# One moving operand of 512 columns for both parts of an activation, and a whole PSUM bank per output tile, in a two-layer decoder trunk

## The chip, the cores and the metric

The kernel runs on one core of a Trainium2 chip. The metric is the device time of one execution in microseconds (us). TensorE (PE in the profile) multiplies, ScalarE (ACT) and VectorE (DVE) do the work on single elements, GpSimd (POOL) builds a few small matrices, and SyncE (SP) issues the transfers. A difference of about 0.2% (1.8 us) is the least that three or more runs of this kernel tell from none.

## The reference

The program is a decoder of two layers over 256 positions and 1024 features. Layer 0 mixes tokens by dilated attention, layer 1 by an mLSTM block. After its mixer every layer runs a squared-ReLU MLP and a gated per-layer embedding:

```
for i in range(DEPTH):
    if i % N_MIXERS == 0:
        x = x + dilated_attention(rms_norm(x, a_norm[j]), ...)     # 9 projections of 1024 x 1024, then w_o
    else:
        x = x + mlstm_mixer(rms_norm(x, b_norm[j]), ...)           # w_up 1024 x 4096, w_down 2048 x 1024
    x = x + squared_relu_mlp(rms_norm(x, mlp_norm[i]), mlp_w1[i], mlp_w2[i])   # relu(h @ w1)**2 @ w2
    gate = jax.nn.sigmoid(rms_norm(x, ple_norm[i]) @ ple_w_gate[i])
    x = x + gate * (p[i] @ ple_w_proj[i])
```

All inputs are fp32, and the result has to be nearly as exact as an fp32 product.

## The kernel before

**Split products.** TensorE works on a short fp32 format (`fp32r`). So each fp32 operand is split into a high part, its rounding, and a low part, the rest, and a product a·w is summed as a_h·w_h + a_l·w_h + a_h·w_l. Weights come from HBM in 138 units of 128 x 2048 (`raw`, 1 MB each). `split` makes `hi` on ScalarE (L176) and `lo` on VectorE (L177), 512 columns at a time. One such piece is called a slot here; a slot holds four weight tiles of 128 x 128, and a unit four slots. `hi` and `lo` are rings of twelve slots, and `split` runs up to 11 slots ahead of the matmuls (`LS`).

**Two kinds of products.** The first 36 units are the attention's q, k and v (`qkv_block`, L499 to L501): there the activation is the stationary operand and 512 weight columns move. The other 102 units are products by `stream`: the weight tile (128 x 128) is stationary and 256 columns of the activation (all positions, features on partitions) move. These 102 units are, in order: proj0 (1 unit), woA and woB (4 together), w1 and w2 of layer 0 (16 each), gate0 (4), xm (8), z0 to z3 (2 each), wd0 (4), proj1 (1), wd1 (4), w1 and w2 of layer 1 (16 each) and gate1 (4). A unit has 16 weight tiles, so there are 1632 of them.

**stream.** For every weight tile it issues three matmuls of 128 x 256 (L331: w_h with a_h; L332: w_h with a_l; L333: w_l with a_h), each with its own weight load. `os` is a pair of output tiles, which share one PSUM bank as `acc[:, 0]` and `acc[:, 1]`; in the last blocks of a few products it is a single tile with half a bank. The pool `psa` has three banks. When a block is done, `done(os, acc)` reads the sum out of PSUM; for pairs that is one operation of 512 columns: `add_x` (wo and wd, L623), `mid` (w1), `fin` (w2, singles), `done` of the gate (L669, held back by `DF` slots for the first outputs, since the norm's factor `rb` is not there yet), `xm_done` (L774) and `done` of z.

**Norms.** `next_h` scales a finished column of x into the next product's activation (`scaled`: `hh` on ScalarE, L298, `hl` on VectorE, L299) and adds its square to the statistics (`Stats`, L264). The factor of the norm is applied after the product, as a row `rb` or `r2` that `rstd_rows` makes six slots (`SB`) into the product.

**Order.** Work that belongs to a later slot is put there by `at`. The order on each engine is made when the kernel is built, by a scheduler that goes by priority: `split` has a low one, `add_x` a high one (`PX`).

Of the kernel before, what the change touches and what calls it, by code (L numbers as in the profile page):

```python
# [39 lines left out]
def _blocks(no, ks, singles=0):  # L40

    n = no - singles
    os = [(o, o + 1) for o in range(0, n, 2)] + [(o,) for o in range(n, no)]
    return [(b, list(ks)) for b in os]

# [94 lines left out]
def _build(ctx, tc, nc, a):  # L140
# [56 lines left out]
    DF = 3  # L197
# [51 lines left out]
    hA = [base.tile([P, KT, S], F32R, name=f"h{n}") for n in "hl"]  # L249
# [68 lines left out]
    def stream(blocks, rhs, done, defer=0):  # L318

        i = 0  # L320
        for os, ks in blocks:
            n = len(os)
            acc = psa.tile([P, n, S], F32, name="acc")
            for k in ks:
                for q, o in enumerate(os):
# [3 lines left out]
                    h, l = rhs(k)  # L329
                    first, last = k == ks[0] and q == 0, k == ks[-1]  # L330
# [12 lines left out]
    def from_h(h):  # L343
        return lambda k: (h[0][:, k], h[1][:, k])
# [730 lines left out]
```

## Time and profile before

| | |
|---|---|
| median of 3 runs | 922.49 us (921.65 to 922.83) |
| the profiled execution | 921.63 us |
| its span, first to last instruction | 919.9 us |
| TensorE busy | 904.3 us, 98% of the span |
| VectorE busy | 659.7 us, 72% |
| ScalarE busy | 569.5 us, 62% |
| mean granted TensorE clock | 0.997 of 2.4 GHz |

The profile shows one execution. A busy time is the time in which at least one instruction of the engine runs; a matmul's duration in it covers the way through the array too, so that consecutive ones overlap, and what a matmul costs in a dense stretch is read from the starts of consecutive ones, not from their durations. For VectorE and ScalarE as well, the next instruction starts about 0.09 us before the one ahead ends.

### The profile page before, as it was taken

How to read it: one execution, taken by the hardware profiler on the slowest of the kernel's cores; microseconds unless marked ns; L12 is line 12 of the kernel's file. 1: busy time of each engine (PE TensorE's matmuls, PEld its weight loads, DVE VectorE, ACT ScalarE, POOL GpSimd, SP SyncE). 2: the span in 40 equal slices, each digit the busy share in tenths (PEclk: the TensorE clock that was granted, in tenths of full speed). 3: DMA queues.
4: the chain of work that ended last, by engine and by line, in shares of the span. 5: the costliest groups of instructions: out<-in, count | busy, mean ns of one | idle time of the engine just before them, and what ended most of it. 6: DMA issues, size and time to landing. Idle time of an engine off the chain costs nothing.

```text
span 919.9 us, 17609 instructions
## 1 busy us (share of the span) xinstructions
PE 904.3 (98%) x6924; PEld 844.3 (92%) x6924; DVE 659.7 (72%) x1409; ACT 569.5 (62%) x1055; POOL 41.5 (5%) x77
## 2 busy tenths in 40 slices
PE   8799999999999999999999999999999999999997
PEld 6687787877889999999999899999999999999997
DVE  6966877857866866665667987568898666656664
ACT  7567576575585766654446686668866666644442
POOL 0400000000000000000000542000000000000000
PEclk9999999999999999999999999999999999999999
DMA  8744443544443555555555433343265555555521
GB/s 302 281 142 160 156 144 133 178 136 145 154 161 105 178 185 183 184 183 184 183 184 183 157 129 104 127 138 98 87 220 204 184 183 184 184 183 182 184 94 46
DMA packets 23122, 150.23 MB, mean 163 GB/s; under 512 B 2560, under 2 KB 3200, under 8 KB 5632
## 3 DMA queue, kind: packets, MB, share of 16 engines
q1 hardware_dynamic: 23040, 149.12, 47.1%
q8 instruction: 54, 0.88, 0.4%
q14 instruction: 28, 0.23, 0.1%
HBM read 148.06 MB, written 1.05 MB: 162 GB/s over the span
## 4 chain that ended last, share of the span: by engine, by line
PE 92%; DVE 6%; ACT 1%; issue 1%; DMA 0%; SPq 0%; ACTq 0%
PE acc L331 21%; PE acc L332 21%; PE acc L333 21%; PE acc L499 6%; PE acc L501 6%; PE acc L500 6%; DVE lo L177 2%; PE tp L451 1%; PE tp L552 1%; PE sm L570 1%; PE sc L527 1%; PE tp L741 1%; PE tp L751 1%; PE sc L882 1%; PE sc L759 1%; PE sc L533 1%
## 5 line engine op out<-in xcount | busy, mean ns | idle before, releaser
L177 DVE TENSOR_TENSOR lo<-raw,hi 128x512 fp32r<-128x512 f32 x552 | 375.6, 691 | 176.7 <-ACT hi L176 175.3
L176 ACT ACTIVATE hi<-raw 128x512 fp32r<-128x512 f32 x552 | 339.2, 628 | 227.1 <-PE acc L332 204.4
L331 PE MATMUL acc<-hh,hi 128*128 128x256 f32 x640 | 184.0, 288 | 0.3 <-ACT hh L298 0.2
L332 PE MATMUL acc<-hl,hi 128*128 128x256 f32 x640 | 181.5, 284 | 0.1
L333 PE MATMUL acc<-hh,lo 128*128 128x256 f32 x640 | 181.4, 283 | 0.0
L331 PE MATMUL acc<-hidh,hi 128*128 128x256 f32 x512 | 144.9, 283 | 0.0
L332 PE MATMUL acc<-hidl,hi 128*128 128x256 f32 x512 | 144.9, 283 | 0.0
L333 PE MATMUL acc<-hidh,lo 128*128 128x256 f32 x512 | 144.9, 283 | 0.0
L331 PEld LDWEIGHTS acc<-hh,hi 128*128 128x128 f32 x640 | 122.4, 191 | 1.6 <-issue 0.7
L332 PEld LDWEIGHTS acc<-hl,hi 128*128 128x128 f32 x640 | 122.5, 191 | 0.7 <-DVE hl L299 0.5
L333 PEld LDWEIGHTS acc<-hh,lo 128*128 128x128 f32 x640 | 122.4, 191 | 0.0
L499 PE MATMUL acc<-hi,hh 128*128 128x512 f32 x264 | 109.6, 416 | 0.0
L500 PE MATMUL acc<-lo,hh 128*128 128x512 f32 x264 | 104.1, 394 | 0.8 <-DVE lo L177 0.8
L501 PE MATMUL acc<-hi,hl 128*128 128x512 f32 x264 | 104.2, 395 | 0.0
L331 PEld LDWEIGHTS acc<-hidh,hi 128*128 128x128 f32 x512 | 98.3, 192 | 0.0
L332 PEld LDWEIGHTS acc<-hidl,hi 128*128 128x128 f32 x512 | 98.3, 192 | 0.0
L333 PEld LDWEIGHTS acc<-hidh,lo 128*128 128x128 f32 x512 | 98.3, 192 | 0.0
L331 PE MATMUL acc<-hBh,hi 128*128 128x256 f32 x320 | 90.9, 284 | 0.0
L332 PE MATMUL acc<-hBl,hi 128*128 128x256 f32 x320 | 90.7, 283 | 0.0
L333 PE MATMUL acc<-hBh,lo 128*128 128x256 f32 x320 | 90.6, 283 | 0.0
L331 PEld LDWEIGHTS acc<-hBh,hi 128*128 128x128 f32 x320 | 61.4, 192 | 0.3 <-issue 0.3
L332 PEld LDWEIGHTS acc<-hBl,hi 128*128 128x128 f32 x320 | 61.4, 192 | 0.0
(258 smaller groups left out, 1384.3 us busy)
## 6 DMA issues: line engine op xcount, KB each, us to landing
raw<-w SPq DMA_DIRECT2D x136, 1024.0 KB, 4.9
raw<-w SPq DMA_DIRECT2D x8, 256.0 KB, 6.8
x<-x SPq DMA_DIRECT2D x4, 256.0 KB, 5.4
pj<-rep SPq DMA_DIRECT2D x1, 896.0 KB, 6.9
out<-u SPq DMA_DIRECT2D x3, 256.0 KB, 2.4
pT<-p SPq DMA_DIRECT2D x2, 256.0 KB, 4.0
nd<-nd SPq DMA_DIRECT2D x1, 384.0 KB, 6.2
out<-u SPq DMA_DIRECT2D x2, 128.0 KB, 1.9
```

The lines of the kernel that those rows point to most:

```text
L176: act(hi[n][:, d], raw[u][:, s], AF.Copy)
L177: dve.tensor_tensor(lo[n][:, d], raw[u][:, s], hi[n][:, d], op=ALU.subtract)
L331: mm(acc[:, q], wh, h, start=first, stop=False, skip_group_check=n > 1)
L332: mm(acc[:, q], wh, l, start=False, stop=False, skip_group_check=n > 1)
L333: mm(acc[:, q], wl, h, start=False, stop=last, skip_group_check=n > 1)
L451: nc.tensor.transpose(ps[:, pair, b * P:(b + 1) * P], n[:, b, ty * 256 + pair * P:ty * 256 + (pair + 1) * P], ident)
L499: mm(accs[b], hh, wh, start=(k == 0), stop=False)
L500: mm(accs[b], hh, wl, start=False, stop=False)
L501: mm(accs[b], hl, wh, start=False, stop=(k == 7))
L527: mm(ps[:, 0:256], q[r, pair, tb], k[r, pair], start=first, stop=last)
L533: mm(ps[64 * e:64 * e + 64, 256 + 64 * n:320 + 64 * n], QT[qt, g][0][r, pair, t4], KTt[qt, g][0][r, pair, t4], start=True, stop=True)
L552: nc.tensor.transpose(psf[:, k * P:(k + 1) * P], pe[:, k * P:(k + 1) * P], ident)
```

## The change

An activation's two parts become one tile with a leading axis of 2 (`parts`): element 0 of what it returns is the whole, 1 the high part, 2 the low part. In `stream` the two matmuls that share w_h become one: w_h is stationary, and both parts move, 2 x 256 columns, into a whole bank; the w_h·a_h sum lands in its first half and the w_h·a_l sum in its second. The third matmul, w_l·a_h, adds to the first half. So each output tile has a bank of its own, and its two halves have to be added when it is read out: `whole` copies the second half to SBUF on ScalarE and adds the first on VectorE, and `add_x` adds one half after the other to x. The blocks are now one pair, whose two banks take turns over k, and then singles (w2 and z: singles alone). Where an operation worked on 512 columns of a pair from PSUM, there is now one of 256 columns per half or per output. In the gate and in xm the read-out no longer waits for `rb`: `whole` is done at once, and the rest (`rest`, `xm_rest`) at slot 6 or later (`late`). Squaring in `mid` moves from ScalarE and VectorE to one VectorE operation (max with 0, times itself), and ScalarE rounds its result. The products of the embeddings (`proj`, 32 weight tiles) keep the old form under the name `stream_pairs`, and q, k and v keep theirs.

```diff
-def _blocks(no, ks, singles=0):
-    n = no - singles
-    os = [(o, o + 1) for o in range(0, n, 2)] + [(o,) for o in range(n, no)]
+def _blocks(no, ks, first=2):
+    os = [tuple(range(first))] + [(o,) for o in range(first, no)]
     return [(b, list(ks)) for b in os]
...
+    def parts(p, name, *shape, **k):
+        t = p.tile([P, 2, *shape], F32R, name=name, **k)
+        return [t, t[:, 0], t[:, 1]]
...
-    def stream(blocks, rhs, done, defer=0):
+    def stream(blocks, h, done):
         i = 0
         for os, ks in blocks:
-            n = len(os)
-            acc = psa.tile([P, n, S], F32, name="acc")
+            accs = [psa.tile([P, 2, S], F32, name="acc") for _ in os]
...
-                    mm(acc[:, q], wh, h, start=first, stop=False, skip_group_check=n > 1)
-                    mm(acc[:, q], wh, l, start=False, stop=False, skip_group_check=n > 1)
-                    mm(acc[:, q], wl, h, start=False, stop=last, skip_group_check=n > 1)
-                    if last and q == n - 1:
-                        if defer and i < 16:
-                            at(clock[0] + defer, done, os, acc)
-                        else:
-                            done(os, acc)
+                    mm(acc.rearrange("p a b -> p (a b)"), wh, h[0][:, :, k], start=first, stop=False, skip_group_check=True)
+                    mm(acc[:, 0], wl, h[1][:, k], start=False, stop=last, skip_group_check=True)
+                    if last:
+                        done(o, acc)
...
+    def late(t0, f, *args):
+        if clock[0] > t0 + SB:
+            f(*args)
+        else:
+            at(t0 + SB, f, *args)
+
+    def whole(out, acc):
+        act(out, acc[:, 1], AF.Copy)
+        dve.tensor_tensor(out, out, acc[:, 0], op=ALU.add)
...
-    def add_x(os, acc):
+    def add_x(o, acc):
         with tc.high_priority(offset=PX):
-            dve.tensor_tensor(x[:, span(os)], x[:, span(os)], acc, op=ALU.add)
+            for n in range(2):
+                dve.tensor_tensor(x[:, o], x[:, o], acc[:, n], op=ALU.add)
...
-            act(u, acc, AF.Relu)
-            s = tmp.tile([P, 2, S], F32, name="s", bufs=2)
-            dve.tensor_tensor(s, u, u, op=ALU.mult)
-            act(hid[0][:, span(os)], u, AF.Square)
-            dve.tensor_tensor(hid[1][:, span(os)], s, hid[0][:, span(os)], op=ALU.subtract)
+            whole(u[:, o % 2], acc)
+            if o % 2:
+                s = tmp.tile([P, 2, S], F32, name="s", bufs=2)
+                dve.scalar_tensor_tensor(s, u, 0.0, u, op0=ALU.max, op1=ALU.mult)
+                act(hid[1][:, o - 1:o + 1], s, AF.Copy)
+                dve.tensor_tensor(hid[2][:, o - 1:o + 1], s, hid[1][:, o - 1:o + 1], op=ALU.subtract)
...
-            dve.tensor_tensor(t, acc[:, 0], r2, op=ALU.mult)
+            whole(t, acc)
+            dve.tensor_tensor(t, t, r2, op=ALU.mult)
...
-            dve.tensor_tensor(t, acc, rb[:, None, :].to_broadcast([P, n, S]), op=ALU.mult)
+            t = tmp.tile([P, S], F32, name="gt", bufs=3)
+            whole(t, acc)
+            late(t0, rest, o, t)
...
-        dve.tensor_tensor(xm, acc, urb[0][:, None, :].to_broadcast([P, 2, S]), op=ALU.mult)
+        whole(xm[:, o % 2], acc)
+        if o % 2 == 0:
+            return
+        late(xm0, xm_rest, o - 1, xm)
```

How the order on the engines changes is shown at three places. The first is TensorE where woB ends and w1 of layer 0 begins. Numbers behind a name tell buffers apart; `oT` is the attention's output, `h` the normed input of w1. Before:

```order
L331 MATMUL acc_3543<-oTh_202,hi_3274 128x256
L332 MATMUL acc_3543<-oTl_203,hi_3274 128x256
L333 MATMUL acc_3543<-oTh_202,lo_3275 128x256
L331 MATMUL acc_3568<-hh_115,hi_3308 128x256 [waits DVE_49,Activation_49]
L332 MATMUL acc_3568<-hl_116,hi_3308 128x256
L333 MATMUL acc_3568<-hh_115,lo_3309 128x256
L331 MATMUL acc_3568<-hh_115,hi_3308 128x256
```

After:

```order
L338 MATMUL acc_3507<-oT_201,hi_3259 128x512
L339 MATMUL acc_3507<-oT_201,lo_3260 128x256
L338 MATMUL acc_3529<-h_115,hi_3292 128x512 [waits DVE_49,PE_49,Activation_49]
L339 MATMUL acc_3529<-h_115,lo_3293 128x256
L338 MATMUL acc_3529<-h_115,hi_3292 128x512 [waits Activation_49]
L339 MATMUL acc_3529<-h_115,lo_3293 128x256
L338 MATMUL acc_3529<-h_115,hi_3315 128x512 [waits DVE_49]
L339 MATMUL acc_3529<-h_115,lo_3316 128x256
L338 MATMUL acc_3530<-h_115,hi_3292 128x512 [waits DVE_49,PE_49]
```

Two matmuls stand for three, the two outputs of the first block have a bank each (3529 and 3530), and the first matmul of a weight tile needs both parts of its column of `h`.

The second place is VectorE at the end of woB: L623 (L656 after) adds a product to x, L299 (L306) makes the low part of `h`, L264 (L271) sums squares, and L177 (L180) is the weights' `lo`. Before:

```order
L177 TENSOR_TENSOR lo<-raw,hi 128x512 [waits Activation_49]
L623 TENSOR_TENSOR x<-x,acc 128x512 [waits PE_49]
L623 TENSOR_TENSOR x<-x,acc 128x256 [waits PE_49]
L299 SCALAR_TENSOR_TENSOR hl<-x,prm,hh 128x256 [waits Activation_49] x2
L264 TENSOR_TENSOR sqa<-sqa,sqt 128x512 [waits Activation_49]
L623 TENSOR_TENSOR x<-x,acc 128x256 [waits PE_49]
L299 SCALAR_TENSOR_TENSOR hl<-x,prm,hh 128x256 [waits Activation_49] x2
```

After:

```order
L656 TENSOR_TENSOR x<-x,acc 128x256 [waits PE_49]
L306 SCALAR_TENSOR_TENSOR h<-x,prm,h 128x256 [waits Activation_49]
L656 TENSOR_TENSOR x<-x,acc 128x256 [waits DVE_49]
L271 TENSOR_TENSOR sqa<-sqa,sqt 128x512 [waits Activation_49]
L306 SCALAR_TENSOR_TENSOR h<-x,prm,h 128x256 [waits Activation_49] x4
L271 TENSOR_TENSOR sqa<-sqa,sqt 128x512 [waits Activation_49]
L180 TENSOR_TENSOR lo<-raw,hi 128x512 [waits DMAHW2_49]
```

Two adds of 256 columns per output stand where one add of 512 served a pair, and the weights' `lo` has moved behind the last `h`.

The third place is VectorE where gate0 ends and xm takes over: L669 (L704 after) multiplies by `rb`, L672 (L707) by the embedding, L697 (L738) adds to x, and L376 is the add of `whole`. Before:

```order
L669 TENSOR_TENSOR u<-acc,rb 128x256 [waits PE_49]
L697 TENSOR_TENSOR xn<-x,u 128x4x4x16 [waits DVE_49]
L177 TENSOR_TENSOR lo<-raw,hi 128x512
L672 TENSOR_TENSOR u<-s,pj 128x256 [waits Activation_49]
L299 SCALAR_TENSOR_TENSOR hl<-xn,prm,hh 128x256 [waits Activation_49]
```

After:

```order
L376 TENSOR_TENSOR gt<-gt,acc 128x256 [waits Activation_49]
L180 TENSOR_TENSOR lo<-raw,hi 128x512
L707 TENSOR_TENSOR gt<-s,pj 128x256 [waits Activation_49]
L704 TENSOR_TENSOR gt<-gt,rb 128x256 [waits DVE_49]
L738 TENSOR_TENSOR xn<-x,gt 128x4x4x16 [waits DVE_49]
```

The read-out of PSUM (L376) has become an operation of its own, ahead of the multiplication by `rb`, for each of the eight outputs.

## Rows read from the trace of the kernel before

**Rows 1.** The page: busy time by engine, and the chain that ended last.
```profile
PE 904.3 (98%) x6924; PEld 844.3 (92%) x6924; DVE 659.7 (72%) x1409; ACT 569.5 (62%) x1055; POOL 41.5 (5%) x77
...
PE 92%; DVE 6%; ACT 1%; issue 1%; DMA 0%; SPq 0%; ACTq 0%
```

**Rows 2.** Timeline of TensorE inside w2, layer 0: start us, us, instruction.
```profile
399.83 0.28 PE L331 MATMUL acc<-hidh,hi 128*128 128x256 f32 x1
...
400.79 0.28 PE L333 MATMUL acc<-hidh,lo 128*128 128x256 f32 x1
```

**Rows 3.** The same in woB, just behind the attention's last pieces.
```profile
294.93 0.28 PE L331 MATMUL acc<-oTh,hi 128*128 128x256 f32 x1
...
295.61 0.28 PE L331 MATMUL acc<-oTh,hi 128*128 128x256 f32 x1
```

**Rows 4.** The same in the q, k, v products, with 512 moving columns.
```profile
190.15 0.39 PE L500 MATMUL acc<-lo,hh 128*128 128x512 f32 x1
...
191.96 0.39 PE L499 MATMUL acc<-hi,hh 128*128 128x512 f32 x1
```

**Rows 5.** Stretches, L332 alone: us, PE, PEld, PEclk, DMA share, GB/s.
```profile
395.15:487.31 92.16, 72.45 (x257) 49.15 (x257) 1.00 0.53 183
293.20:301.90 8.70, 6.98 (x26) 4.69 (x25) 1.00 0.60 218
190.00:194.00 4.00, 0.00 (x0) 0.00 (x0) 1.00 0.81 270
```

**Rows 6.** Stretches by product, busy us of PE, PEld, DVE, ACT, POOL; PEclk, DMA, GB/s.
```profile
302.00:395.15 93.15, 93.15 (x777) 93.15 (x778) 67.96 (x111) 58.54 (x102) 0.00 (x0) 1.00 0.53 182
395.15:487.31 92.16, 92.16 (x771) 92.16 (x770) 55.26 (x89) 46.00 (x76) 0.00 (x0) 1.00 0.53 183
487.31:511.23 23.92, 23.92 (x202) 23.92 (x201) 20.20 (x48) 16.62 (x30) 0.00 (x0) 1.00 0.39 133
511.23:581.94 70.71, 69.11 (x526) 66.20 (x525) 56.30 (x119) 49.90 (x99) 28.62 (x52) 1.00 0.40 138
581.94:648.25 66.31, 66.09 (x512) 63.55 (x511) 48.48 (x131) 47.00 (x83) 0.00 (x0) 1.00 0.38 128
648.25:676.81 28.56, 28.56 (x230) 27.82 (x229) 25.66 (x71) 23.10 (x40) 0.00 (x0) 1.00 0.33 112
676.81:682.89 6.08, 6.08 (x54) 6.08 (x53) 6.06 (x12) 4.54 (x9) 0.00 (x0) 1.00 0.55 220
682.89:705.93 23.04, 23.04 (x195) 23.04 (x194) 20.41 (x35) 15.59 (x29) 0.00 (x0) 1.00 0.67 229
```

**Rows 7.** Timeline of VectorE in wd1: instructions that follow without a gap.
```profile
684.45 4.30 DVE L177 TENSOR_TENSOR lo<-raw,hi 128x512 fp32r<-128x512 f32 x7
...
690.11 0.89 DVE L299 SCALAR_TENSOR_TENSOR hBl<-xn,prm,hBh 128x256 fp32r<-128x256 f32 x2
...
703.76 0.42 DVE L623 TENSOR_TENSOR xn<-xn,acc 128x256 f32<-128x256 f32 x1
704.10 0.68 DVE L177 TENSOR_TENSOR lo<-raw,hi 128x512 fp32r<-128x512 f32 x1
```

**Rows 8.** Groups by form: busy us, mean ns of one, idle before.
```profile
L658 DVE TENSOR_TENSOR u<-acc,rb 128x256 f32<-128x256 f32 x16 | 6.8, 425 | 2.4 <-PE acc L333 0.4
...
L294 ACT ACTIVATE rb<-sm 128x256 f32<-128x256 f32 x5 | 1.9, 382 | 6.5 <-PE sm L293 6.5
```

**Rows 9.** Timeline of gate0 into xm: VectorE's first L669, two adds to x.
```profile
499.24 1.36 DVE L669 TENSOR_TENSOR u<-acc,rb 128x512 f32<-128x512 f32 x2
...
510.36 1.09 DVE L697 TENSOR_TENSOR xn<-x,u 128x256 f32<-128x256 f32 x2
```

**Rows 10.** Timeline of the end: TensorE's last matmul, VectorE's first and last operation behind.
```profile
914.91 0.28 PE L333 MATMUL acc<-hh,lo 128*128 128x256 f32 x1
915.23 0.42 DVE L669 TENSOR_TENSOR u<-acc,rb 128x256 f32<-128x256 f32 x1 [1.02 <-PE acc L333]
...
916.66 0.42 DVE L978 TENSOR_TENSOR u<-xn,u 128x256 f32<-128x256 f32 x1
```

More of the change, by code (lines that the diff above doesn't have):

```diff
@@ L247, in pr @@
         return prm[:, o:o + w]
-    hA = [base.tile([P, KT, S], F32R, name=f"h{n}") for n in "hl"]
+    hA = parts(base, "h", KT, S)
     sqp = pool("sq", 2)
@@ L341, in stream, with stream_pairs @@
                     i += 1
-    def from_h(h):
-        return lambda k: (h[0][:, k], h[1][:, k])
+    def stream_pairs(blocks, h, done):
+        i = 0
+        for os, ks in blocks:
+            acc = psa.tile([P, 2, S], F32, name="acc")
+            for k in ks:
+                for q, o in enumerate(os):
+                    if i % 4 == 0:
+                        u, c = open_slot()
+                    wh, wl = weights(u, (i % 16) * P, P)
+                    first, last = k == ks[0] and q == 0, k == ks[-1]
+                    mm(acc[:, q], wh, h[1][:, k], start=first, stop=False, skip_group_check=True)
+                    mm(acc[:, q], wh, h[2][:, k], start=False, stop=False, skip_group_check=True)
+                    mm(acc[:, q], wl, h[1][:, k], start=False, stop=last, skip_group_check=True)
+                    if last and q == 1:
+                        done(os, acc)
+                    if i % 4 == 3:
+                        close_slot()
+                    i += 1
+    def late(t0, f, *args):
[6 more added lines that the diff above has]
+        dve.tensor_tensor(out, out, acc[:, 0], op=ALU.add)
     actx = ExitStack()
@@ L422, in _build @@
     at(44, small_products)
-    oT = [atp.tile([P, KT, S], F32R, name=f"oT{n}") for n in "hl"]
+    oT = parts(atp, "oT", KT, S)
     QT, KTt, VT = {}, {}, {}
@@ L674, in gate, with rest, done @@
-        stream(B_GATE, from_h(h2), done, DF)
+        def rest(o, t):
+            dve.tensor_tensor(t, t, rb, op=ALU.mult)
+            g = tmp.tile([P, 2, S], F32, name="s", bufs=2)[:, 0]
+            act(g, t, AF.Sigmoid)
+            dve.tensor_tensor(t, g, pj[:, o], op=ALU.mult)
+            finish(o, t)
+        t0 = clock[0]
+        def done(o, acc):
+            t = tmp.tile([P, S], F32, name="gt", bufs=3)
+            whole(t, acc)
+            late(t0, rest, o, t)
+        stream(B_GATE, h2, done)
@@ L676, in _build @@
     mctx = ExitStack()
     mp = pool("mlp0", c=mctx)
-    hid = [mp.tile([P, 32, S], F32R, name=f"hid{n}") for n in "hl"]
+    hid = parts(mp, "hid", 32, S)
     hgp = pool("hG", c=xctx0, side="right")
-    hG = [hgp.tile([P, KT, S], F32R, name=f"hG{n}") for n in "hl"]
+    hG = parts(hgp, "hG", KT, S)
     gst = Stats()
@@ L687, in _build @@
     xn = xp1.tile([P, KT, S], F32, name="xn")
-    hB = [xp1.tile([P, KT, S], F32R, name=f"hB{n}") for n in "hl"]
+    hB = parts(xp1, "hB", KT, S)
     mctx = ExitStack()
@@ L876, in memory @@
         nums = []
+        sq = zp.tile([P, 2, 512], F32, name="nsq")
         ss = None
@@ L884, in memory @@
             nums.append(ps)
[L885 removed]
+            t = sq[:, j]
             act(t, ps, AF.Square)
@@ L972, in _build, with finish1 @@
     mp = pool("mlp1", c=mctx)
-    hid = [mp.tile([P, 32, S], F32R, name=f"hid{n}") for n in "hl"]
+    hid = parts(mp, "hid", 32, S)
     gst = Stats()
     mlp(1, x, hB, mst, hid, mp, hA, "gP1", gst)
-    def finish1(os, t):
-        dve.tensor_tensor(t, x[:, span(os)], t, op=ALU.add)
-        nc.sync.dma_start(a["out"][:, span(os)], t)
+    def finish1(o, t):
+        dve.tensor_tensor(t, x[:, o], t, op=ALU.add)
+        nc.sync.dma_start(a["out"][:, o], t)
     gate(1, hA, gst, mp, finish1)
```

139 lines of the change are left out of this document (71 added, 68 removed).

## The prediction

> **What bounds the kernel now.** First the page: TensorE is busy for 98% of the span, and the chain that ended last is 92% TensorE, 6% VectorE [rows 1]. So TensorE's pace decides, and the first question is what sets it. A matmul's duration (0.28 us) doesn't say; the distance between starts does. Inside w2 nine starts of 256-column matmuls lie 0.96 us apart in sum, 0.120 us each [rows 2]. In woB, just behind the attention, seven starts lie 0.68 us apart, 0.113 us each, with the same operation and the same shape [rows 3]. In the q, k, v products nine starts of 512-column matmuls lie 1.81 us apart, 0.226 us each, which is twice 0.113 [rows 4].
>
> So the array can take 256 columns every 0.113 us and does so when matmuls have piled up in front of it; in the long streams it takes one every 0.120 us. I read the 0.120 as the pace at which a weight load and its matmul are handed to the array: it does not depend on the columns, and behind 512-column matmuls (0.226) or a stall there is a stock to draw on. Memory traffic isn't the cause: the transfers moved 183 GB/s where the pace was 0.120, but 218 and 270 GB/s where it was 0.113 and 0.226 [rows 5]. Nor is it the clock, which is at its upper level, 2.4 GHz (granted 1.00), in all three. The second question is what the other engines have left, since the change gives them work: VectorE is busy 73% of w1 and 60% of w2, but 84% of gate0, 80% of xm, 90% of wd0, 100% of proj1 and 89% of wd1 [rows 6].
>
> **The change part by part.** *TensorE.* A weight tile took three loads and three matmuls, 3 x 0.120 = 0.360 us. It now takes two loads and two matmuls. Handing over asks for 2 x 0.120 = 0.240; the columns ask for 0.226 + 0.113 = 0.340 [rows 3, 4]. The larger counts: 0.340, 0.020 less. The form changes for 1600 of the 1632 tiles; the 64 of woA and woB partly ran at 0.113 already, so I count 1536 x 0.020 = 30.7 us. What no row shows is a moving operand in two runs of 256 columns that lie apart. I take it as free, the nearest row being the 512 in one run; at worst a run costs a 256-column matmul's 0.120 and the gain is nothing.
>
> The Trainium skill ("TensorE: Matmul & The Clock Gate", section "Back-to-back issue gap") speaks against this change: it gives a distance of N/2.4 + 2.5 ns between full-speed matmuls, so columns cost the same however they are divided. By it a tile would take 327.5 ns before and 325.0 after, an estimate of 4 us for 1600 tiles in place of 30.7. Its 109 ns for 256 columns stands against 120 in w2, so the trace disagrees there, and against 113 in woB, where it comes near.
>
> *Prices on VectorE and ScalarE.* Seven `lo` in a row take 4.30 us, so 512 columns occupy VectorE for (4.30 - 0.69)/6 = 0.60 us; a 256-column add from PSUM 0.34 (703.76 to 704.10); a scaled subtraction of 256 about 0.40 (0.89 for two) [rows 7]. ScalarE's 256-column copy out of PSUM lasts 0.38 us, VectorE's 256-column operation on PSUM 0.43 [rows 8]. So `whole` costs VectorE 0.34 us per output, two for every pair that was one of 0.60 or none.
>
> *w1, w2.* Per pair of outputs in w1 VectorE has four `lo` (2.40), two adds (0.68), the new max-multiply and the subtraction (0.60 each): 4.3 us in 16 x 0.340 = 5.44 us, 79%. In w2 per output: eight `lo` (4.8), three operations of 256 (1.0), 0.40 and half a square sum (0.3): 6.5 of 10.9 us. A bank is wanted again two outputs after its own (5.4 us in w1), and read-out takes about 1 us. So these four products, 1024 tiles, stay with TensorE, and nothing is added there. If VectorE's cover were gone in w1 the excess over 5.44 us per pair would be paid 32 times.
>
> *woB into w1.* woB has two k per output: 16 tiles, 5.4 us. VectorE has 16 adds (5.5), eight low parts (3.2) and four square sums (2.4), 11.1 us, in place of 3 x 0.60 + 2 x 0.34 + 5.6 = 8.1. The `lo` are put behind it in the new order. TensorE needs the last column of `h` only 14 tiles into w1: 5.4 + 4.8 = 10.2 us, and three banks let it run two outputs ahead. Bounds 0 and 5.5 (all adds on the path); I take 1.5, near the excess of 11.1 over 10.2 plus one add from PSUM.
>
> *gate0 into xm.* VectorE's first operation with `rb` started 11.9 us into gate0 [rows 9]; with slots 0.08 us shorter, six of them ahead, it is 11.4. Behind it the new order has, up to the last low part, eight times 0.34 + 0.34 + 0.54 + 0.40 + 0.30 (15.4 us; 0.54 is the add to x, 1.09 for two [rows 9]), five `whole` adds (1.7) and about five `lo` (3.0): it ends at 31.5. TensorE has gate0's 64 tiles (21.8), eight small matmuls (0.9, what gate0's 23.92 us leave over 64 x 0.360) and, by the new order, 18 tiles of xm that need only the first six columns (6.1): 28.8. It waits 2.7 us, and more for the links over ScalarE; before it idled 1.6 us in xm (70.71 - 69.11) [rows 6]. Net 2; bounds 0 and 6 (the links' own time with no tile to fill).
>
> *xm to wd1.* From 511.23 to 705.93 us VectorE is busy 56.30 + 48.48 + 25.66 + 6.06 + 20.41 = 156.9 us [rows 6]. Added are 32 adds of `whole` in xm and z (10.9) and, in wd0 and wd1, 32 adds (10.9) for seven of 0.60 and two of 0.34 (4.9): 16.9 in sum. TensorE's 194.7 us lose 384 x 0.020 = 7.7. That makes 173.8 of 187.0 us, 93%. But wd0 has 25.66 + 5.44 - 2.40 = 28.7 in 27.3 us, and wd1 20.41 + 5.44 - 2.48 = 23.4 in 21.8. The excess, 1.4 + 1.6 = 3.0 us, is the value I take. Below it, 0: `lo` runs up to 11 slots (15 us) ahead and can give way. Above, 16.9, if all of it came to the path.
>
> *The end.* Before, the last matmul started at 914.91, VectorE read PSUM at 915.23 and ended its work at 917.08 [rows 10]. A copy by ScalarE (0.38), an add (0.43) and a hand-over (some 0.1) come in between: 0.9 us.
>
> *Sum.* -30.7 + 1.5 + 2 + 3.0 + 0.9 = -23.3 us. Against the profiled execution, 921.63, that is 898.3. The median is 0.86 above that execution: **899.2 us**. With every waiting cost but the end's at 0 it is 891.8 + 0.9 = 892.7; with woB at 5.5 and gate0 at 6 it is 907.2.
>
> **The rivals.** *A, columns set the pace (slower).* If 0.120 us is what 256 columns cost in the long streams and woB's 0.113 is the exception, a tile takes 0.240 + 0.120 = 0.360 as before. The gain is 0 and the waits (7.4) stay: 921.63 + 7.4 + 0.86 = 929.9. It decides from a pace of 0.355 us per tile on, where 1536 tiles give back less than 7.4 us. For it: 0.120 holds through all of w1 and w2. Against it: rows 4 with transfers at their busiest. The skill's rule on the gap leads here too, since it lets columns cost the same in any division.
>
> *B, a step in between.* The joined matmul may pay for its second run, or the 256 behind it may stay at 0.120: one step of 0.007 makes 0.347, a gain of 20 us and 909.9; two make 0.353, a gain of 10 us and 920. For it: no row has two runs. Against it: 0.113 and 0.226 are in the ratio of their columns.
>
> *C, VectorE becomes the bound from xm to wd1.* Half of the 16.9 us and half of the upper bounds at woB and gate0 come to the path: 8.5 + 2.8 + 3 + 0.9 = 15.2, so 921.63 - 30.7 + 15.2 + 0.86 = 907.0. For it: 100% in proj1 and 90% around it [rows 6]. Against it: the 15 us of lead.
>
> *D, the work doesn't shrink.* The order shows two matmuls where three stood, throughout, so this has next to no chance.
>
> **How the numbers follow.** My case (892.7 to 907.2) 0.65; C 0.12; B at 909.9 0.10, at 920 0.05; A 0.08. The range 891 to 913 takes in my case, nearly all of C (one in four of it lies beyond) and B's first step: 0.65 + 0.09 + 0.10 = 0.84. Faster by over 0.2% (below 920.6) are my case, C, B's first step and the half of its second: 0.65 + 0.12 + 0.10 + 0.02, less 0.01 for a C with all of the 16.9 us: 0.88. Within 0.2%, which is about what a measurement of this kernel can tell from no change, are the other half and that C: 0.04. Slower is A: 0.08.
>
> **What would show it.** In w2 after, starts of matmuls should alternate at 0.226 and 0.113 us, and w2 should last 256 x 0.340 = 87.0 us in place of 92.16; 0.360 per tile means A, 0.347 B. VectorE in w1 should be near 79% busy with TensorE never waiting. TensorE's idle time should stand at the start of w1 in layer 0, at k = 6 and 7 in xm, and between z3 and w1 of layer 1, some 7 us in sum; 15 us or more means C. The prediction is wrong above all if the pace in w2 isn't 0.340.

## The result: 917.06 us, 0.6% faster, a quarter of what was forecast

| | before | after |
|---|---|---|
| median of the runs, us | 922.51 | 917.06 (916.03 to 918.22) |
| ratio after / before | | 0.9943, 95% interval 0.9925 to 0.9960 |
| span of the profiled execution, us | 919.86 | 915.3 |

The change gained 5.5 us where 23.3 were forecast, and the time lies above the range (891 to 913). In the page of the changed kernel, the busy line and the chain that ended last:

```profile
PE 893.8 (98%) x5324; PEld 757.6 (83%) x5324; DVE 708.1 (77%) x1598; ACT 588.1 (64%) x1158; POOL 41.5 (5%) x77
...
PE 87%; DVE 9%; ACT 1%; issue 1%; DMA 1%; SPq 0%; ACTq 0%
```

Against [rows 1], 1600 matmuls have gone, as the change says, but TensorE's busy time fell by 10.5 us only and its share of the chain by five points, four of which went to VectorE and a transfer. The stretches by product, in program order (the columns are those of [rows 6]):

```profile
303.28:394.56 91.28, 91.28 (x523) 79.30 (x521) 79.23 (x146) 59.26 (x117) 0.00 (x0) 1.00 0.52 185
394.56:485.01 90.45, 90.45 (x515) 78.46 (x513) 56.80 (x98) 47.21 (x83) 0.00 (x0) 1.00 0.53 186
485.01:510.39 25.38, 24.08 (x138) 20.45 (x137) 22.31 (x61) 19.34 (x41) 0.00 (x0) 1.00 0.37 126
510.39:580.10 69.71, 68.03 (x399) 58.87 (x397) 61.22 (x136) 53.08 (x115) 28.33 (x52) 1.00 0.40 139
580.10:645.77 65.67, 65.55 (x386) 56.62 (x385) 51.12 (x142) 53.08 (x100) 0.00 (x0) 1.00 0.32 113
645.77:677.77 32.00, 29.66 (x168) 25.68 (x167) 28.93 (x85) 22.48 (x41) 0.00 (x0) 0.95 0.33 112
...
706.01:795.84 89.83, 89.83 (x523) 78.60 (x522) 77.23 (x139) 57.92 (x113) 0.00 (x0) 1.00 0.57 199
795.84:884.58 88.74, 88.74 (x514) 77.60 (x513) 56.70 (x98) 47.19 (x83) 0.00 (x0) 1.00 0.51 178
884.58:915.34 30.76, 24.09 (x138) 20.25 (x136) 19.67 (x57) 11.79 (x26) 0.00 (x0) 0.94 0.10 35
```

These are w1, w2, gate0, xm, z, wd0, and layer 1's w1, w2 and gate. TensorE is busy for all of w1 and w2, and the waits listed below are none of theirs; yet w2 lasts 90.45 and 88.74 us, not the 87.0 that the prediction asked for, and the two layers differ though they run the same program of 256 tiles. The four MLP stages together took 10.2 us less than the 370.5 of before. All the rest lost 5.7 us, though its tiles too have one matmul less: gate0 1.5, wd0 3.4, gate1 2.0, woA and woB 1.5, while xm gained 1.0.

How a tile's time is made up, from TensorE's timeline in w2 of layer 0 and then of layer 1 (start us, us, instruction):

```profile
449.68 0.40 PE L338 MATMUL acc<-hid,hi 128*128 128x512 f32 x1
449.92 0.28 PE L339 MATMUL acc<-hid,lo 128*128 128x256 f32 x1
450.03 0.40 PE L338 MATMUL acc<-hid,hi 128*128 128x512 f32 x1
...
450.74 0.40 PE L338 MATMUL acc<-hid,hi 128*128 128x512 f32 x1
```

```profile
829.81 0.39 PE L338 MATMUL acc<-hid,hi 128*128 128x512 f32 x1
...
830.50 0.39 PE L338 MATMUL acc<-hid,hi 128*128 128x512 f32 x1
```

In layer 0 three tiles take 450.74 - 449.68 = 1.06 us, 0.353 each; in layer 1 two take 830.50 - 829.81 = 0.69 us, 0.345 each by these rounded starts, and 88.74/256 = 0.3467 over the stage. Neither is 0.340, and neither wanders: each of the two stages keeps its pace. What TensorE waited for most, over the whole part from woB on (engine and line, what it waited for: us in sum, times, longest):

```profile
PE acc L338 <- DVE hB L975: 1.8, 1, 1.8
PE acc L338 <- DVE gt L376: 1.8, 2, 1.2
PE acc L338 <- DVE x L656: 0.8, 2, 0.5
PE acc L338 <- DVE h L306: 0.7, 1, 0.7
```

They are the new waits: wd0 on the last columns of its operand, both gates on the read-out of a bank (`whole`, L376), woB on the add to x, which empties a bank, and xm on the last columns of h. In the kernel before, the same list has 0.2 us for xm's `h` and none of the others.

### The profile page after: what moved, and what is told of

Its sections match the earlier page's. It is cut to its first block, busy times and chain, and to the rows that moved or that the text cites. A ratio compares the mean times of both kernels' runs of the same rounds, so it can differ in the third digit from the quotient of the medians.

```text
span 915.3 us, 14689 instructions
## 1 busy us (share of the span) xinstructions
PE 893.8 (98%) x5324; PEld 757.6 (83%) x5324; DVE 708.1 (77%) x1598; ACT 588.1 (64%) x1158; POOL 41.5 (5%) x77
## 4 chain that ended last, share of the span: by engine, by line
PE 87%; DVE 9%; ACT 1%; issue 1%; DMA 1%; SPq 0%; ACTq 0%
PE acc L338 37%; PE acc L339 19%; PE acc L531 7%; PE acc L533 6%; PE acc L532 6%; DVE lo L180 3%; PE tp L483 1%; PE tp L584 1%; PE sm L602 1%; PE sc L559 1%; PE sc L800 1%; PE sc L935 1%; PE sc L565 1%; PE tp L792 1%; PE tp L782 1%
## 5 line engine op out<-in xcount | busy, mean ns | idle before, releaser
L180 DVE TENSOR_TENSOR lo<-raw,hi 128x512 fp32r<-128x512 f32 x552 | 373.9, 690 | 132.7 <-ACT hi L179 130.0
L338 PE MATMUL acc<-h,hi 128*128 128x512 f32 x640 | 229.8, 402 | 1.3 <-DVE h L306 0.7
L339 PE MATMUL acc<-h,lo 128*128 128x256 f32 x640 | 179.7, 281 | 0.0
L338 PE MATMUL acc<-hid,hi 128*128 128x512 f32 x512 | 179.3, 396 | 0.0
L338 PEld LDWEIGHTS acc<-h,hi 128*128 128x128 f32 x640 | 120.2, 188 | 30.4 <-DVE h L306 1.0
L339 PE MATMUL acc<-hid,lo 128*128 128x256 f32 x512 | 142.8, 279 | 0.0
L339 PEld LDWEIGHTS acc<-h,lo 128*128 128x128 f32 x640 | 120.8, 189 | 0.3
L338 PE MATMUL acc<-hB,hi 128*128 128x512 f32 x320 | 113.8, 400 | 1.8 <-DVE hB L975 1.8
L531 PE MATMUL acc<-hi,h 128*128 128x512 f32 x264 | 109.8, 416 | 0.0
L532 PE MATMUL acc<-lo,h 128*128 128x512 f32 x264 | 104.2, 395 | 0.8 <-DVE lo L180 0.8
L533 PE MATMUL acc<-hi,h 128*128 128x512 f32 x264 | 104.3, 395 | 0.0
L533 PEld LDWEIGHTS acc<-hi,h 128*128 128x128 f32 x264 | 50.0, 189 | 11.1
L531 PEld LDWEIGHTS acc<-hi,h 128*128 128x128 f32 x264 | 50.2, 190 | 9.5
L376 DVE TENSOR_TENSOR u<-u,acc 128x256 f32<-128x256 f32 x80 | 33.2, 415 | 0.5 <-ACT u L375 0.3
```

The lines of the kernel that those rows point to most:

```text
L180: dve.tensor_tensor(lo[n][:, d], raw[u][:, s], hi[n][:, d], op=ALU.subtract)
L338: mm(acc.rearrange("p a b -> p (a b)"), wh, h[0][:, :, k], start=first, stop=False, skip_group_check=True)
L339: mm(acc[:, 0], wl, h[1][:, k], start=False, stop=last, skip_group_check=True)
L376: dve.tensor_tensor(out, out, acc[:, 0], op=ALU.add)
L531: mm(accs[b], hh, wh, start=(k == 0), stop=False)
L532: mm(accs[b], hh, wl, start=False, stop=False)
```

## The experiments

Two readings stood against each other. The **hand-over reading** is the prediction's: a load with its matmul is handed over every 0.120 us whatever its columns, and the columns alone need 0.113 per 256. The **fixed-cost reading** was formed on the traces after: each load with its matmul takes its columns at 2.4 GHz and some 13 ns besides, so that leaving out one of three saves those 13 ns, or 7, and not 20. The "changed kernel" in the texts below is the kernel after.

### What a load with its matmul costs by itself

Behind the changed kernel's last matmul come rows of matmuls on hid's data; each has another weight tile, and no result is used. From the second row on no other engine is at work; in the first, VectorE, ScalarE and a transfer still end the kernel's own work. A row has one width, or a repeated pattern of widths ("two" is the operand of two runs, as in the change):

```
+    def probe(kinds, reps, same=False):
...
+            for w, q in kinds:
+                st = line[:, (i % 48) * P:(i % 48) * P + P] if not same else line[:, 0:P]
+                mv = hid[0][:, :, 8 + r % 16] if w == "two" else line[:, 6144:6144 + w]
+                out = flat[q][:, 0:512 if w == "two" else w]
+                mm(out, st, mv, start=(r == 0), stop=(r == reps - 1), skip_group_check=True)
...
+    probe([(256, 0)], 60)
+    probe([("two", 0), (256, 0)], 60)
...
```

> The changed kernel with a row of 900 extra matmuls on hid's data behind its last one, while nothing else runs, so that the pace of a load with its matmul is seen alone for each width; their results are not used, and the kernel's own time is not the point. Fixed-cost theory (each load with its matmul takes its columns at 2.4 GHz plus about 13 ns, give or take a step of 7): widths of 256, 512, 384, 192, 128 columns start 120, 227, 173, 93 and 67 ns apart, a 512 with a 256 takes 347 (or 340, or 353), whether the 512 are one run or two. Hand-over theory of the prediction (0.120 us is the least pace of a load with its matmul; columns 0.227 for 512 only when they are longer): 120, 227, 173 for the widths above 256, but 120 for 192 and 128 too, and 340 or 347 for the pair. Theory that the operand of two runs costs a step: the pair with one run of 512 takes 340, with two runs 347 or more. Theory that ScalarE's and VectorE's traffic slows it in the kernel: 340 for both here, against the 347 and 353 in the kernel.

The stretches, each from the first start of a row to the first of the next. In order: 60 matmuls of 256 columns; 60 pairs of "two" and 256; 60 pairs of 512 in one run and 256; 60 of 512; 60 of 384; 60 of 192; 60 of 128; and, behind a row that is left out here, 30 times two of 512 and two of 256 in that order, about from where the clock was up again. Columns as in [rows 6]; a count takes in the instructions that reach into the stretch:

```profile
909.83:917.01 7.18, 7.18 (x62) 7.18 (x61) 2.28 (x6) 1.11 (x3) 0.00 (x0) 1.00 0.11 37
917.01:938.21 21.20, 21.20 (x122) 18.39 (x121) 0.00 (x0) 0.00 (x0) 0.00 (x0) 1.00 0.00 1
938.21:959.41 21.20, 21.20 (x122) 18.39 (x121) 0.00 (x0) 0.00 (x0) 0.00 (x0) 1.00 0.00 1
959.41:973.04 13.63, 13.63 (x62) 11.28 (x61) 0.00 (x0) 0.00 (x0) 0.00 (x0) 1.00 0.01 1
973.04:983.47 10.43, 10.43 (x62) 10.43 (x61) 0.00 (x0) 0.00 (x0) 0.00 (x0) 1.00 0.00 0
983.47:990.14 6.67, 6.67 (x61) 6.67 (x61) 0.00 (x0) 0.00 (x0) 0.00 (x0) 1.00 0.01 2
990.14:996.81 6.67, 6.67 (x62) 6.67 (x61) 0.00 (x0) 0.00 (x0) 0.00 (x0) 1.00 0.00 0
...
1010.20:1029.20 19.00, 19.00 (x111) 16.59 (x110) 0.00 (x0) 0.00 (x0) 0.00 (x0) 0.99 0.00 0
```

Divided by the matmuls, this is 120, 227 and 174 ns for 256, 512 and 384 columns, and 111 for both 192 and 128. From 256 to 512 columns the distance grows by 227 - 120 = 107 ns, which is 256 columns at 2.4 GHz; so in these rows each matmul costs its columns and 13.3 ns (120 - 106.7). A row of 256 columns near the end of the probe, with every other engine idle, settled at 120 too. For fewer columns there is a floor of 111 ns, which I put down to the load, since it no longer depends on the moving columns; no row varies the load, so this isn't shown. This is the fixed-cost reading, with a floor that it didn't have: I had expected 93 and 67 ns for 192 and 128. The hand-over reading needs the floor at 120 and 256 columns at 113; the first is 9 ns less, the second 7 more in these rows. That 256 columns can also go at 113 for long is taken up below, where the prediction is gone through.

A pair takes 21.20/60 = 353 ns, with one run or with two, and with nothing else on the chip's engines. So neither the two runs nor VectorE's and ScalarE's traffic makes the 353. Two of 512 ahead of two of 256 take 348 ns per pair in their steady state (two cycles in turn of 698 and 695 ns); this row comes back below.

The Trainium skill ("TensorE: Matmul & The Clock Gate", section "LDWEIGHTS (loading the stationary operand)") gives the weight load's columns divided by 1.2 GHz, an estimate of 106.7 ns for 128 columns. The floor of 111 ns agrees within 5 ns at the upper clock. In the row that is left out, of 64 columns, matmuls came 111 to 112 ns apart as long as the clock was granted 1.00; then it fell to its lower level (granted 0.50), with TensorE running on without a stop, and they came 213 ns apart, which that estimate doesn't give.

### The join taken apart

```
-mm(acc.rearrange("p a b -> p (a b)"), wh, h[0][:, :, k], start=first, stop=False, skip_group_check=True)
+mm(acc[:, 0], wh, h[1][:, k], start=first, stop=False, skip_group_check=True)
+mm(acc[:, 1], wh, h[2][:, k], start=False, stop=False, skip_group_check=True)
```

> The changed kernel with its 512-column matmul taken apart again into two of 256 on the two halves of the same bank; layout, bank, read-out and order stay as changed. Fixed-cost theory: all stages of the two layers return to 0.360 us a tile, w1 and w2 to about 92.2 us, and the time is before's 922.5 plus what the new read-out costs, 930 to 934 (the pace alone was worth 13 to 16 us). If the read-out costs nothing and the join only gained the 5.5 us that were measured: 922 to 924. Prediction's terms (30.7 us from the join, 7.4 us lost): 948 if the join had been worth that, which the changed kernel's stages already deny.

935.83 us, ratio 1.0142 (1.0126 to 1.0159). So the join is worth 18.8 us, and the rest of the change (bank, read-out, order) costs 12.9. Its w1 and w2 of layer 0, and wd0:

```profile
304.30:397.42 93.12, 93.12 (x776) 93.12 (x777) 79.22 (x145) 58.89 (x116) 0.00 (x0) 1.00 0.53 181
397.42:489.58 92.16, 92.16 (x770) 92.16 (x769) 56.93 (x98) 47.21 (x83) 0.00 (x0) 1.00 0.54 183
...
650.79:687.28 36.49, 32.71 (x240) 30.72 (x239) 32.03 (x89) 23.50 (x44) 0.00 (x0) 0.95 0.33 112
```

w1 and w2 of layer 0 are what they were in [rows 6] to 0.03 us: there the new read-out costs TensorE nothing, although VectorE is busy 85% of w1. The 12.9 us lie elsewhere, 7.9 of them in wd0 alone (28.56 before). So not all of the 18.8 us is pace: the four MLP stages make 10.5 of it, and wd0, with longer waits, some time at the lower clock (0.95 in the mean) and its own 64 tiles, another 4.5.

### One run of 512 columns

```
-t = p.tile([P, 2, *shape], F32R, name=name, **k)
-return [t, t[:, 0], t[:, 1]]
+t = p.tile([P, shape[0], 2, shape[1]], F32R, name=name, **k)
+return [t, t[:, :, 0], t[:, :, 1]]
...
```

> The changed kernel with the two parts of an activation tile laid next to each other, so that the 512 columns are one run of 2 KB instead of two runs of 1 KB far apart; all else stays. Fixed-cost theory: the pace stays at 0.347 or 0.353 us a tile, the time within 3 us of 917. Theory that two runs cost a step: 0.340 in w1 and w2, 87.0 us a stage, 905 to 910.

917.74 us (0.9929 to 0.9959), the same as the changed kernel; its w2 stages:

```profile
394.08:484.53 90.45, 90.45 (x514) 78.39 (x513) 56.80 (x98) 47.20 (x83) 0.00 (x0) 1.00 0.53 186
...
795.33:884.07 88.74, 88.74 (x514) 77.60 (x513) 56.69 (x98) 47.20 (x83) 0.00 (x0) 1.00 0.51 178
```

To 0.01 us as after. That the operand lies in two runs costs nothing here; the prediction was right to take it as free.

### The two paces

The kernel of the next section (the joined operand in w1 and w2 alone), with one extra matmul of another width ahead of every sixteenth tile of both w2.

```
+if len(blocks) == 8 and k % 16 == 0:
+    w = NUDGE.pop(0)
+    mm(nb[:, 0:w], wl, h[0].rearrange("p a b -> p (a b)")[:, 0:w], start=True, stop=True)
```

> The kernel with the joined operand in w1 and w2 alone, with one extra matmul of 64 to 512 columns on scratch ahead of every sixteenth tile of both w2, another width each time; their results are not used. If the two paces (353.3 and 346.7 ns a tile) are two phases in which a row of matmuls runs on, the rows behind different widths fall into one or the other and stay there up to the next extra matmul: some of the 32 rows at 346.7. If the pace belongs to a stage, an address or the neighbouring engines' traffic: all 32 at 353.3. The extra matmuls take 5 us together in either case, 917 to 921 us.

921.69 us in its one run. The widths went from 64 to 512 in 32 values. Fourteen of the 32 rows ran at 346.7 ns a tile, eighteen at 353.3, and none changed on its way. Two neighbours, behind extra matmuls of 256 and of 264 columns (timeline of TensorE; the last row of each is twelve tiles behind the one above it):

```profile
422.67 0.28 PE L365 MATMUL tp<-hid,lo 128*128 128x256 f32 x1
...
423.14 0.39 PE L366 MATMUL acc<-hid,hi 128*128 128x512 f32 x1
...
427.30 0.39 PE L366 MATMUL acc<-hid,hi 128*128 128x512 f32 x1
...
428.34 0.28 PE L365 MATMUL tp<-hid,lo 128*128 128x264 f32 x1
...
429.15 0.40 PE L366 MATMUL acc<-hid,hi 128*128 128x512 f32 x1
...
433.39 0.40 PE L366 MATMUL acc<-hid,hi 128*128 128x512 f32 x1
```

The first twelve tiles take 4.16 us, 0.3467 each, the second 4.24, 0.3533. So the pace isn't a matter of the stage, the addresses or the traffic alone: a row of matmuls falls into one of two phases at its start and stays in it until something interrupts it. Which one it falls into follows no order of widths that I could find. What the phase is locked to, no run shows.

### The join where TensorE sets the pace alone

The kernel before with the joined operand, whole bank and read-out in w1 and w2 of both layers, everything else as before:

```
-stream(B_W1, from_h(h1), mid)
+stream_joined(B_W1, h1, mid)
...
-stream(B_W2, from_h(hid), fin)
+stream_joined(B_W2, hid, fin)
```

> The kernel before with the joined operand, the whole bank and the new read-out in the four stages w1 and w2 of both layers alone; gates, attention, xm, z and the projections down keep three matmuls of 256 columns and their old order. Fixed-cost theory: each of 1024 tiles saves 6.7 or 13.3 ns, so 7 to 14 us less with no new waits outside the four stages: 909 to 916, under the changed kernel's 917. If waits in w1 and w2 eat it (the read-out's extra VectorE work): 916 to 922. Prediction's pace of 0.340: 902, with w1 and w2 at 87 us.

914.35 us (0.9885 to 0.9926), 2.7 under the changed kernel, with 576 tiles fewer joined. Its w2 of layer 0:

```profile
393.82:484.27 90.45, 90.45 (x514) 78.46 (x513) 56.72 (x98) 47.20 (x83) 0.00 (x0) 1.00 0.53 187
```

In the profiled run (915.81 us) all four MLP stages fell into the slower phase (w2 90.45 in both layers), and it is still ahead: outside w1 and w2 the change as a whole loses.

### The order within two tiles, and within four

The same kernel, with the tiles of w1 and w2 taken two at a time: both 512-column matmuls, then both of 256.

```
+for two in zip(tiles[0::2], tiles[1::2]):
...
+    for (k, q, o), w in zip(two, ws):
+        mm(accs[q].rearrange("p a b -> p (a b)"), w[0], h[2][:, :, k], start=k == ks[0], stop=False, skip_group_check=True)
+    for (k, q, o), w in zip(two, ws):
+        mm(accs[q][:, 0], w[1], h[0][:, k], start=False, stop=k == ks[-1], skip_group_check=True)
```

> The kernel with the joined operand in w1 and w2 alone (914.4 us), its instructions taken two tiles at a time there: 512, 512, 256, 256 columns in place of 512, 256, 512, 256. The row of bare matmuls took 348.3 ns a tile in that order against 353.4. If that pace holds among the kernel's other work: w1 and w2 at 89.2 to 90.0 us, 909 to 911. If a tile's time is one more 512 and one more 256 whatever the order: 914 as it was. If the read-out is worse placed: over 915.

910.62 us (0.9858 to 0.9887). The w2 stages of layers 0 and 1:

```profile
392.12:481.29 89.17, 89.17 (x515) 77.80 (x513) 56.66 (x97) 47.19 (x83) 0.00 (x0) 1.00 0.54 189
...
790.36:879.53 89.17, 89.17 (x514) 77.80 (x513) 56.66 (x97) 47.17 (x83) 0.00 (x0) 1.00 0.50 177
```

89.17/256 = 0.3483 us a tile, as the bare row had promised, and the same in both layers: this order has no second pace to fall into in the stages seen. Four at a time (`zip` over four tiles in place of two):

> The kernel with the joined operand in w1 and w2 alone, its instructions taken four tiles at a time there: four of 512 columns, then four of 256. If a 512 behind a 512 and a 256 behind a 256 go at the pace of their own rows (226.8 and 120.0 ns) and only the change of width costs more: 346.8 to 347.6 ns a tile, w1 and w2 at 88.8 to 89.8 us, 908.5 to 910.5. If the order of two at a time already gave all (348.3): 910 to 911.5.

913.69 us (0.9892 to 0.9925); its w2 of layer 0:

```profile
392.82:482.64 89.82, 89.82 (x515) 78.52 (x514) 56.68 (x97) 47.01 (x83) 0.00 (x0) 1.00 0.53 188
```

That is 0.351 a tile: worse than two at a time, where I had expected it a little better. Behind another width, 512 and 256 columns don't keep the pace of their own rows: within a group of four the 512s start 232 to 234 ns apart in the mean, not 227. Which sequence of widths is best has to be tried.

### More stages joined, and the best kernel

The joined operand also in xm, z and wd1, beside w1 and w2; gates, woA, woB and wd0 as before:

```
-stream(B_XM, from_h(hA), xm_done, DF)
+stream_joined(B_XM, hA, xm_done)
...
-stream(B_Z, from_h(hA), done)
+stream_joined(B_Z, hA, done)
...
+if n:
+    stream_joined(B_WD[n], hA, done1)
```

> The joined operand in w1 and w2, and also in xm, z and the second half of the projection down; the gates, the attention's projections and the first half down keep three matmuls of 256. In the changed kernel xm, z1 and the second half down were 1.0, 0.3 and 0.4 us shorter, z0 0.3, and z2 with z3 the same. If these gains stand when the waits of gate 0 ahead of them are gone: 911 to 913.5. If the read-out's VectorE work makes the first half down late as in the changed kernel (32.0 us against 28.6 of before): 914 to 918.

912.10 us (0.9849 to 0.9925), its runs from 907.6 to 914.7. In its profile xm lasts 68.84 us (70.71 before), wd0 29.24 (28.56). The MLP of layer 0 fell into the quick phase there (w2 88.74) and that of layer 1 into the other (90.45); if the phase differs from run to run, with 1.6 us or so on each of four stages, that would make its wide spread. That isn't shown, since only one run of a kernel has a trace.

The same with the order in twos (both edits together):

> The order 512, 512, 256, 256 and the joined operand together in w1, w2, xm, z and the second half of the projection down; the rest in three matmuls of 256. If the two gains add (910.6 us with the order in w1 and w2 alone, and the other stages 2.0 us shorter in the profile of the kernel that joined them too): 907.5 to 910, with less spread between runs than that kernel showed (907.6 to 914.7), since the order's pace of 348.3 did not depend on the phase. If the order makes the read-outs of two tiles collide in xm and z: 911 or more.

909.27 us, ratio 0.9858 (0.9843 to 0.9873), its runs within 0.6 us of each other. It is the lowest time found: 13.2 us under the kernel before, 7.8 under the changed one. From the order in w1 and w2 alone (0.9858 to 0.9887) the runs don't tell it apart. xm, then wd0:

```profile
506.25:574.91 68.66, 68.00 (x399) 58.80 (x397) 60.36 (x134) 52.84 (x115) 28.46 (x52) 1.00 0.41 142
...
640.68:669.92 29.24, 28.71 (x228) 27.72 (x227) 27.57 (x73) 22.85 (x41) 0.00 (x0) 1.00 0.43 153
```

### Two of the new waits

The last gate. In the changed kernel 0.85 us pass from TensorE's start at 902.57 to its next; ScalarE's copy out of the bank waits there for a transfer of the output out of a `gt` buffer (ScalarE's waits from 898 to 904 us: 3.9 us in sum, 3.7 the longest).

```
-dve.tensor_tensor(t, x[:, o], t, op=ALU.add)
-nc.sync.dma_start(a["out"][:, o], t)
+dve.tensor_tensor(x[:, o], x[:, o], t, op=ALU.add)
+nc.sync.dma_start(a["out"][:, o], x[:, o])
```

> The changed kernel with the last gate's result written over x's tile instead of over gt, so that no gt buffer waits for the transfer of the output out of it. If the gap of 0.85 us at 902.6 us is that wait: no gap there, the last gate 0.8 us shorter than 30.8 and the time some 916 us, apart from which of its two paces each stage falls into. If the gap comes of something else on ScalarE's queue: it stays, and the last gate at 30.8.

The stop is gone and the last gate lasts 29.89 us in place of 30.76. The time, 916.56 us (0.9924 to 0.9953), doesn't tell it from the changed kernel; in the profiled run layer 1's MLP fell into the slower phase (w2 90.45), which took more than the gain. In this run wd0 had the same stop as after, 2.10 us, but lasted 30.39 us: behind it the clock stayed at 1.00, while in the changed kernel's profile TensorE was granted 0.59 (the lower level for most of 4.17 us), as the stretches of its wd0 show, from the first tile to the stop, the stop, and behind it:

```profile
645.77:649.13 3.36, 2.85 (x18) 2.24 (x16) 3.26 (x9) 2.86 (x4) 0.00 (x0) 1.00 0.00 0
649.13:651.23 2.10, 0.28 (x3) 0.00 (x1) 2.10 (x7) 2.08 (x5) 0.00 (x0) 1.00 0.28 43
651.23:655.40 4.17, 4.17 (x14) 3.54 (x15) 4.13 (x15) 4.13 (x8) 0.00 (x0) 0.59 0.58 230
```

So of wd0's 3.4 us, some 1.6 are the clock behind the stop (32.00 - 30.39); the same stop of 2.10 us came with the fall of the clock in one profile and without it in the other. What makes the stop? In the kernel before, wd0's two outputs lay in one bank, and their tiles ran in turn. In two banks they are two separate chains, and in the changed kernel the seventh tile of wd0 already asks for hB's last columns, as it does when the first six all belong to one output. The next kernel puts wd0 back to three matmuls and two outputs in a bank.

```
...
-stream(B_WD[n], hA if n else hB, done)
...
+if n:
+    stream(B_WD[n], hA, done)
+else:
+    stream_pairs(B_WD[n], hB, done_pair)
```

> The changed kernel with the first half of the projection down (wd0) alone put back: three matmuls of 256 columns, two outputs in one bank, one add of 512 columns for both. In the changed kernel wd0 lasts 32.0 us against 28.6 of before, with a stop of 2.1 us on hB's last columns at 649.1 us. If that is the order (two outputs in two banks are two separate chains, TensorE's row runs one of them ahead and asks for the last columns at its seventh tile, not at its thirteenth): the stop shrinks to 0.2 to 0.8 us and wd0 is 28.8 to 29.8 us, as in the kernel that had wd0 in pairs beside joined z. If it is VectorE's surplus of work in wd0 and z (the prediction's reading): a stop on hB of 2 us stays wherever the order asks for it, wd0 at 31 us or more.

wd0 lasts 29.23 us. What TensorE waits for around its start, and when VectorE makes hB's last columns, first in the changed kernel, then in this one:

```profile
PE acc L358 <- DVE hB L975: 0.3, 1, 0.3
PE acc L357 <- ACT hB L974: 0.2, 1, 0.2
...
650.49 0.68 DVE L975 TENSOR_TENSOR hB<-mt,hB 128x512 fp32r<-128x512 f32 x1
...
651.18 0.69 DVE L975 TENSOR_TENSOR hB<-mt,hB 128x512 fp32r<-128x512 f32 x1 [0.17 <-ACT hB L974]
```

VectorE is done with hB no earlier here, 5.8 us into wd0 (646.03) against 5.4 in the changed kernel (645.77); TensorE asks for it later, at its thirteenth tile. So the order was the cause of the stop, not VectorE's surplus of work; with the stop the loss of clock is gone too (1.00). Yet the time is 918.03 us (0.9918 to 0.9961), no better, though one of its seven runs took 911.57: in the profiled run w1 and w2 of layer 1, behind it, went from 89.83 and 88.74 us to 91.38 and 90.45, the slower phase, and lost 3.3 us against the 2.8 gained:

```profile
646.03:675.26 29.23, 28.71 (x228) 27.71 (x227) 27.52 (x73) 22.88 (x41) 0.00 (x0) 1.00 0.43 145
704.19:795.57 91.38, 91.38 (x522) 79.30 (x521) 75.41 (x136) 57.84 (x113) 0.00 (x0) 1.00 0.53 185
795.57:886.02 90.45, 90.45 (x515) 78.39 (x513) 56.70 (x98) 47.19 (x83) 0.00 (x0) 1.00 0.50 175
```

## Why the prediction was wrong, point by point

**The bound** was right. TensorE sets the time, and w1 and w2 stayed with it: no wait appeared in them, and taking the join out gave their old lengths back. VectorE's share in w1 came to 87%, not 79%, without harm.

**The pace, the step that failed.** "I read the 0.120 as the pace at which a weight load and its matmul are handed to the array", and from it 0.340 us a tile and -30.7 us. A tile takes 0.3533 or 0.3467, which is 0.007 or 0.013 less than before and not 0.020. The four MLP stages gained 10.2 us for 1024 tiles, 10 ns a tile, and at that rate the 1536 tiles that were counted make some 15 us. This term alone is 15 of the 18 us by which the forecast missed. The bare rows show why. 0.120 is what 256 columns cost with one load (106.7 + 13.3), and 0.226 in [rows 4] what 512 cost with one (213.3 + 13.3): the same fixed part at both widths, with no need of a stock of matmuls ahead. Two stretches at the same width had two paces, and I gave the lower one to the columns because 0.226 was twice it; 0.120 + 0.107 would have fitted [rows 2] and [rows 4] just as well and would have given 0.347.

It would not have fitted [rows 3], and those seven starts are no accident of a few matmuls: 38 of the 64 tiles of woA and woB took 0.340 us in three matmuls, 17 of them between the first two lines below, from the trace before. The changed kernel's tiles there mostly took 0.353, eleven of them between the last two lines:

```profile
292.89 0.28 PE L331 MATMUL acc<-oTh,hi 128*128 128x256 f32 x1
...
298.67 0.28 PE L331 MATMUL acc<-oTh,hi 128*128 128x256 f32 x1
...
294.28 0.40 PE L338 MATMUL acc<-oT,hi 128*128 128x512 f32 x1
...
298.17 0.40 PE L338 MATMUL acc<-oT,hi 128*128 128x512 f32 x1
```

With the join taken apart again, 33 of these 64 tiles took 0.353 or 0.354 in three matmuls, 0.118 each. So matmuls of 256 columns alone have more than one lasting pace too, 0.113, 0.118 and 0.120, and the fixed part is 13.3 ns at the slowest of them and 6.7 at the quickest. Where the three matmuls ran at 0.113, the join lost 13 ns a tile and gained nothing; what it gains is the difference between the paces that a stage falls into before and after. Why a stage falls into one or the other stays open.

**Rival A** was half right: 0.120 is what 256 columns cost in the long streams. Its conclusion, no gain at all, failed, since the cost has a fixed part that the join saves once per tile. The Trainium skill's rule ("TensorE: Matmul & The Clock Gate", section "Back-to-back issue gap"), columns at 2.4 GHz plus a constant, has the form that the bare rows show; its constant of 2.5 ns stands against 13.3 there. The section gives that rule for the isolated gap of a single matmul, not for a stream of loads and matmuls, which the prediction didn't say. **Rival B** is what happened, both of its steps, each in its own stages. It had 0.15, and the 909.9 to 920 that its two steps span held the result, though the waits came to about 11 us where it had 7.4. One of its reasons for a step, the second run of the operand, was wrong: one run made no difference. The other, the 256 behind it at 0.120, fits the quicker pace (0.227 + 0.120). **Rival C** did not happen: from xm to wd1 VectorE was busy 168.7 of 195.6 us, 86%, and most of the waiting there had another cause (below). **Rival D**: the 1600 matmuls went, as the order said.

**woB into w1** (1.5): woA and woB lasted 1.5 us more. The size is right by luck: TensorE stopped in woB itself, twice, for banks that VectorE hadn't yet added to x, and not at the start of w1 for the last column of `h`; some 0.4 us of it is the slower pace above, a cost that the prediction put at nothing for these tiles. **gate0 into xm** (2): gate0 and xm together came out 0.46 us longer, and 192 tiles at 10 ns less hide another 1.9; so about 2.4 us of waiting. Right in size; but half of it stands in gate0 itself, where a bank waits for its read-out behind the operations with `rb`, which the prediction had placed in xm alone. **xm to wd1** (3.0 from VectorE's surplus): z, wd0, proj1 and wd1 came out 1.9 us longer, with some 2.5 us of pace gained, so 4.4 us of waiting. The size is near by luck, for the cause was another: 2.8 us of it was wd0's order and the lower clock behind its stop, which the wd0 experiment removed with VectorE's work in z and wd1 as it was. That clock is a price that a stop can have and that the sum didn't hold. **The end** (0.9): the last matmul to the end of the span went from 4.95 to 6.38 us, 1.4; with the wait on the output's buffer and the bank's read-out the last gate lost 2.0, and about 2.6 with its pace taken out. Too small, for a wait that wasn't seen. In sum the waits, with woB's slower pace, are about 11 us in place of 7.4.

## What to carry to other kernels

A pace read from one width says nothing about what the width costs: two widths are needed, in rows of equal length and history, and the difference between them is the columns' price and the rest the instruction's. And if one width shows two paces, both have to be explained, or both carried into the range. Joining two matmuls into one saved the fixed part alone, here 7 to 13 ns of 120 (and lost 13 where the three had run at their quickest), so it pays only where the new read-out is hidden. The lowest time had the join in such stages only, with 512-column matmuls in twos. When two accumulators that shared a bank get banks of their own, their chains come apart, and the order in which operands are asked for can change with them.

## What was not expected of the hardware

A steady row of alternating 512- and 256-column matmuls has two lasting paces, 346.7 and 353.3 ns a pair, and a row keeps the one it has until something interrupts it; in one stage of 256 tiles that is 1.7 us, and in one profile it ate up the gain of a repaired wait. A row of 256 columns alone ran for long at 113, 118 or 120 ns a matmul. At the clock's lower level (granted 0.50) the fixed part is gone: in the bare rows 512 columns came 426.5 ns apart and 256 columns 213.5, which is the columns at 1.2 GHz and nothing more. And 192 columns cost as much as 128, 111 ns, in a row with a weight load for each.
